# SwiGLU: two plain blocks' weights asked for before the first product's blocks, and the second product's weights asked for nine pieces ahead

## The chip, the cores and the metric

The kernel runs on one core of a Trainium2 chip, in one launch. The metric is the device time of that core in microseconds. Before the change three runs took 1242.67, 1244.71 and 1245.03 us, median 1244.71 us. A further execution was profiled: it took 1243.57 us, and its records span 1241.0 us; every row below is from that one.

## The reference

The model is a trunk of two layers on 512 positions of 1024 features in float32: a recurrent mixer (RG-LRU) with a SwiGLU, then a dilated windowed attention with a second SwiGLU. The change touches the two SwiGLUs alone, each of which computes, with a hidden width of 2816:

```python
def swiglu(h, w_in, w_out):
    g, u = jnp.split(h @ w_in, 2, axis=-1)
    return (jax.nn.silu(g) * u) @ w_out

h = h + swiglu(rms_norm(h, a_ffn_norm[i]), a_ffn_w_in[i], a_ffn_w_out[i])
```

## The kernel before

**Engines.** TensorE (PE) multiplies. Each float32 product is done as three matmuls of 128x512 (L163, L164, L165) on operands that were split into a high and a low part: a weight piece lands in a raw tile wr, ScalarE (ACT) casts the high part into wh (L117), and VectorE (DVE) subtracts to get the low part wl (L124). SyncE (SP) issues nearly all loads and GpSimd (POOL) the adding loads; both, like ACT and DVE, work through their instructions in the written order.

**The stream of pieces.** All weights are one list of pieces, numbered through the whole program. `ws.get(i)` hands out the split parts of piece i; before that, `prefetch(i)` asks for the loads of all pieces up to i + `al`, and splits all up to i + `asp`. There are two raw tiles wr and three pairs wh, wl; so the load of a piece waits until the piece two loads before it has been split, and its split waits until PE has finished with the piece three before it. `load_to(i)` asks for loads up to piece number i of the whole program and does nothing when they have been asked for.

**One SwiGLU** (`swiglu`, called for both layers, f1 and f2). Of the hidden blocks, two (four pieces: two gates, two ups) go the plain way; I call these plain pieces p0 to p3 in their order. The other 20 go through a scheme of seven products in five rounds, q0 to q4, whose raw weights lie in tiles GA, GB, S1, S3 and UB that `fetch` loads (two loads of 512 KB each; S1 and S3 get a second pair, added by POOL, L638). The text ORDERS says in which order the products (GA.B11 and so on), the blocks of the second product ("O", weights f_out) and the split of the round before's results ("L", `parts_of`) stand. In q1 to q3 it is S1, GA, GB, L, S2, O, O, S3, O, S4, O, UB. I call the four second-product pieces of a round O1 to O4. A product takes two pieces of the list (they have no load of their own, since they are split from GA and the like), an O one. `land` (L718) moves a round's results with 16 small DMAs after UB.

**At the start** of a SwiGLU, p0 and p1 were already asked for by the stage before. The normalization needs the sum of squares ssum (L288), which PE adds up (L296) after p0; DVE makes a reciprocal root and diagonals dgh and dgl from it (L298 to L308); PE spreads them over the partitions (L314, L315) after p1; ACT copies the result, rb (L316), and then p2, p3 and GA follow on PE. The block of code around L776 to L788 writes the order of SP, ACT, DVE, POOL and PE by hand, except that splits have a higher priority and may be placed earlier. The tiles of `fetch` lie where the stage before had its own, so the first fetch waits for the end of that stage's work (ssum).

## Time and profile before

| | PE | DVE | ACT | POOL |
|---|---|---|---|---|
| busy, us | 1167.8 | 852.6 | 624.4 | 189.3 |
| share of the span (1241.0 us; this execution's time 1243.57 us) | 94% | 69% | 50% | 15% |

The two SwiGLUs lie at about 151 to 510 us and 862 to 1241 us of the span. The page gives, for each engine, its busy time, and for each pair of instruction and cause how long the engine sat idle until that cause came. A time is worth something only where PE, the busiest engine, waits; so the idle time of PE and its clock are what to look at. Matmuls overlap: one of 128x512 is listed with 0.39 us but the next starts some 0.23 us later.

### The profile page before, as it was taken

What the parts mean: (1) busy time and instruction counts of PE and PEld (TensorE: products, weight loads), DVE (VectorE), ACT (ScalarE), POOL (GpSimd) and SP (SyncE); (2) the same over time, 40 slices, a digit from 0 to 9 for tenths busy, and PEclk for the clock granted to TensorE, in tenths of its full rate; (3) what the DMA queues carried; (4) which work ended last, traced back from release to release, by engine and by line L of the source; (5) the groups of instructions that cost most, each with busy time, mean ns of one, the idle gap of its engine ahead of it and who ended that gap; (6) DMA issues with size and microseconds to landing.
All of it is one profiled execution on the core that took longest, in us unless ns stands there. A gap on an engine that the chain in (4) does not pass through costs nothing.

```text
span 1241.0 us, 15125 instructions
## 1 busy us (share of the span) xinstructions
PE 1167.8 (94%) x5403; PEld 960.5 (77%) x5403; DVE 852.6 (69%) x1525; ACT 624.4 (50%) x901; POOL 189.3 (15%) x221
## 2 busy tenths in 40 slices
PE   9999929999999999999999999999299999999998
PEld 6788827878787788888888888898278787878887
DVE  8987527886757587787564676756378667675864
ACT  6796315553524353575555677645255535352522
POOL 4210010110101000010411343340101101010000
PEclk9999979999999999999999999999699999999999
DMA  7643190884655632432978567434808756465324
GB/s 242 133 119 106 64 288 1 218 237 123 192 147 175 164 103 63 124 112 89 226 178 177 128 142 165 98 72 106 252 20 226 195 153 186 132 181 146 106 70 130
DMA packets 92234, 179.61 MB, mean 145 GB/s; under 512 B 8704, under 2 KB 27008, under 8 KB 92160
## 3 DMA queue, kind: packets, MB, share of 16 engines
q1 hardware_dynamic: 72144, 130.23, 31.8%
q0 software_dynamic: 18864, 47.19, 21.6%
q10 hardware_dynamic: 1152, 1.23, 0.3%
q8 instruction: 43, 0.70, 0.2%
q14 instruction: 31, 0.25, 0.1%
HBM read 164.99 MB, written 2.10 MB: 135 GB/s over the span
## 4 chain that ended last, share of the span: by engine, by line
PE 78%; DVE 8%; DMA 7%; ACT 4%; issue 2%; SPq 1%; POOL 0%; ACTq 0%; DVEq 0%
PE ps L164 21%; PE ps L165 21%; PE ps L163 20%; PE ps L1031 5%; PE ps L1032 5%; PE ps L1033 5%; DMA wr<-in_f_out 3%; DMA wr<-in_f_in 2%; DVE wl L653 1%; DMA GB<-in_f_in 1%; ACT wh L117 1%; ACT wh L652 1%; PE ps L1110 1%; PE ps L1197 1%; DVE xc L449 1%
## 5 line engine op out<-in xcount | busy, mean ns | idle before, releaser
L117 ACT CAST wh<-wr 128x1024 fp32r<-128x1024 f32 (+2 forms) x136 | 131.7, 969 | 191.7 <-PE ps L164 83.4
L124 DVE TENSOR_TENSOR wl<-wr,wh 128x1024 fp32r<-128x1024 f32 (+2 forms) x93 | 100.5, 1084 | 80.4 <-ACT wh L117 80.0
L163 PE MATMUL ps<-gh,wh 128*128 128x512 f32 x288 | 117.3, 407 | 14.5 <-ACT wh L117 14.5
L164 PE MATMUL ps<-wl,xh 128*128 128x512 f32 x320 | 125.0, 391 | 1.9 <-DVE wl L653 1.9
L163 PE MATMUL ps<-wh,xh 128*128 128x512 f32 x320 | 124.7, 390 | 0.0
L165 PE MATMUL ps<-wh,xl 128*128 128x512 f32 x320 | 124.6, 390 | 0.0
L164 PE MATMUL ps<-gl,wh 128*128 128x512 f32 x288 | 118.1, 410 | 0.8 <-issue 0.5
L165 PE MATMUL ps<-gh,wl 128*128 128x512 f32 x288 | 118.0, 410 | 0.1
L638 POOL DMA_DIRECT2D S<-in_f_in x40 | 48.4, 1270 | 420.1 <-DMA S<-in_f_in 140.2
L163 PE MATMUL ps<-xh,wh 128*128 128x512 f32 x256 | 102.3, 401 | 0.8 <-ACT xh L274 0.8
L164 PE MATMUL ps<-xl,wh 128*128 128x512 f32 x256 | 101.2, 395 | 0.1
L652 ACT CAST wh<-S 128x1024 fp32r<-128x1024 f32 x60 | 63.0, 1050 | 75.6 <-PE ps L164 30.3
L165 PE MATMUL ps<-xh,wl 128*128 128x512 f32 x256 | 100.9, 394 | 0.0
L653 DVE TENSOR_TENSOR wl<-S,wh 128x1024 fp32r<-128x1024 f32 x60 | 73.1, 1222 | 32.7 <-ACT wh L652 32.7
L165 PE MATMUL ps<-wh,T 128*128 128x512 f32 x240 | 93.5, 390 | 0.0
L164 PE MATMUL ps<-wl,T 128*128 128x512 f32 x240 | 93.5, 390 | 0.0
L163 PE MATMUL ps<-wh,T 128*128 128x512 f32 x240 | 93.5, 390 | 0.0
L1031 PE MATMUL ps<-wh,xh 128*128 128x512 f32 x224 | 91.5, 408 | 0.0
L1033 PE MATMUL ps<-wh,xl 128*128 128x512 f32 x224 | 87.7, 392 | 0.0
L1032 PE MATMUL ps<-wl,xh 128*128 128x512 f32 x224 | 87.4, 390 | 0.0
L769 DVE TENSOR_TENSOR h<-h,ps 128x512 f32<-128x512 f32 x64 | 43.5, 686 | 60.8 <-PE ps L165 60.8
L163 PEld LDWEIGHTS ps<-gh,wh 128*128 128x128 f32 x288 | 56.2, 195 | 29.6 <-ACT wh L117 17.1
(284 smaller groups left out, 2684.9 us busy)
## 6 DMA issues: line engine op xcount, KB each, us to landing
S<-in_f_in SPq DMA_DIRECT2D x40, 512.0 KB, 4.6
S<-in_f_in POOLq DMA_DIRECT2D x40, 512.0 KB, 7.5
wr<-in_f_out SPq DMA_DIRECT2D x36, 512.0 KB, 5.7
wr<-in_w_q SPq DMA_DIRECT2D x28, 512.0 KB, 6.8
wl<-in_w_q POOLq DMA_DIRECT2D x28, 512.0 KB, 7.5
GA<-in_f_in SPq DMA_DIRECT2D x20, 512.0 KB, 4.5
GB<-in_f_in SPq DMA_DIRECT2D x20, 512.0 KB, 4.6
UB<-in_f_in SPq DMA_DIRECT2D x20, 512.0 KB, 5.9
```

The source lines that it names most:

```text
L117: nc.scalar.copy(hi[:, c], r[:, c])
L124: a = eng.tensor_tensor(lo[:, c], r[:, c], hi[:, c].bitcast(F32), ALU.subtract)
L163: PE.matmul(ps, wh, xh, start=first, stop=False, skip_group_check=on)
L164: PE.matmul(ps, wh, xl, start=False, stop=False, skip_group_check=on)
L165: PE.matmul(ps, wl, xh, start=False, stop=last, skip_group_check=on)
L638: nc.gpsimd.dma_start(c, p.part(1, q, n == "S1", i), accum_op=ALU.add)
L652: S.copy(hi, r)
L653: V.tensor_tensor(lo, r, hi.bitcast(F32), ALU.subtract)
L769: V.tensor_tensor(by_time(x), by_time(x), in_turn(ps), ALU.subtract)
L1031: PE.matmul(ps[t], xh[k][:, r], wh[:, c], start=k == 0, stop=False)
L1032: PE.matmul(ps[t], xh[k][:, r], wl[:, c], start=False, stop=False)
L1033: PE.matmul(ps[t], xl[k][:, r], wh[:, c], start=False, stop=k == 7)
```

## The change

`load_to` gets the numbers of p2 and p3, where it had 2 and 3, numbers of the whole list that had long been loaded. So p2 is asked for ahead of GA, and p3 between GA and GB. Loads are asked for nine pieces ahead, and four again from the first product of the last round on.

```diff
         def swiglu(fp, p, after, meanwhile=iter(())):
-            ws.asp, ws.al = 2, 4
+            ws.asp, ws.al = 2, 9
...
             with tc.manual_schedule(engines={E.PE, E.DVE, E.Activation, E.SP, E.Pool}):
-                ws.load_to(2)
+                ws.load_to(p.steps[2][3])
                 fetch(0, "GA")
-                ws.load_to(3)
+                ws.load_to(p.steps[3][3])
                 for n in ("GB", "S1", "S3", "UB"):
                     fetch(0, n)
                 for s, (kind, *what) in enumerate(p.steps):
+                    if kind == "product" and what[0] == len(ORDERS) - 1:
+                        ws.al = 4
                     {"plain": plain_block, "product": product, "out": out_block, "parts": parts_of}[kind](*what)
```

First place: SP at the start of f1. wr_1291 and wr_1328 are p0 and p1, the next two loads from f_in into wr are p2 and p3; S_ is S1, then S3. Before:

```order
L100 DMA wr_1291<-in_f_in 128x1024
L100 DMA wr_1328<-in_f_in 128x1024
L636 DMA GA<-in_f_in 128x2x512 x2
L636 DMA GB<-in_f_in 128x2x512 x2
L636 DMA S_1387<-in_f_in 128x2x512 x2
L636 DMA S_1392<-in_f_in 128x2x512 x2
L636 DMA UB<-in_f_in 128x2x512 x2
L100 DMA wr_1401<-in_f_in 128x1024
L100 DMA wr_1403<-in_f_in 128x1024
L93 DMA wr_1600<-in_f_out 128x4x256
```

And of the changed kernel, at the same place of SP:

```order
L100 DMA wr_1291<-in_f_in 128x1024
L100 DMA wr_1328<-in_f_in 128x1024
L100 DMA wr_1381<-in_f_in 128x1024
L636 DMA GA<-in_f_in 128x2x512 x2
L100 DMA wr_1386<-in_f_in 128x1024
L636 DMA GB<-in_f_in 128x2x512 x2
L636 DMA S_1391<-in_f_in 128x2x512 x2
L636 DMA S_1396<-in_f_in 128x2x512 x2
L636 DMA UB<-in_f_in 128x2x512 x2
L93 DMA wr_1405<-in_f_out 128x4x256
```

p2 and p3 have moved from behind the ten loads of fetch to places before GA and behind it; round q0's first second-product piece follows directly. SP has the same difference at the start of f2.

Second place: DVE at the end of the stage ahead of f1. h_71 is the last of the eight tiles of the residual stream. Before:

```order
L533 TENSOR_TENSOR h_71<-h_71,ps 128x512
L275 SCALAR_TENSOR_TENSOR xl<-h_71,par,xh 128x512
L288 TENSOR_TENSOR ssum<-ssum,sq 128x512
L124 TENSOR_TENSOR wl_1410<-wr_1401,wh_1409 128x1024
L595 TENSOR_TENSOR wt<-h_64 128x256
```

And changed:

```order
L533 TENSOR_TENSOR h_71<-h_71,ps 128x512
L124 TENSOR_TENSOR wl_1412<-wr_1381,wh_1411 128x1024
L275 SCALAR_TENSOR_TENSOR xl<-h_71,par,xh 128x512
L288 TENSOR_TENSOR ssum<-ssum,sq 128x512
L595 TENSOR_TENSOR wt<-h_64 128x256
```

The split of p2 has moved ahead of the last low part xl and the last addition to ssum; on ACT its cast has moved ahead of the last xh in the same way. The rest of DVE, ACT, POOL and PE stands in the same order in both kernels.

Third place: SP from the end of round q0 through q1 of f1. The gl rows are `land`, GA and the rest the fetches for q2, the wr rows O1 to O4 of q1. Before:

```order
L718 DMA gl<-wt 32x4x128 x12
L636 DMA GA<-in_f_in 128x2x512 x2
L636 DMA S_2066<-in_f_in 128x2x512 x2
L93 DMA wr_2088<-in_f_out 128x2x512
L93 DMA wr_2106<-in_f_out 128x2x512
L93 DMA wr_2180<-in_f_out 128x2x512
L636 DMA S_2220<-in_f_in 128x2x512 x2
L93 DMA wr_2272<-in_f_out 128x2x512
L636 DMA GB<-in_f_in 128x2x512 x2
```

And changed:

```order
L93 DMA wr_1949<-in_f_out 128x2x512
L718 DMA gl<-wt 32x4x128 x12
L93 DMA wr_1991<-in_f_out 128x2x512
L636 DMA GA<-in_f_in 128x2x512 x2
L93 DMA wr_2065<-in_f_out 128x2x512
L636 DMA S_2072<-in_f_in 128x2x512 x2
L93 DMA wr_2144<-in_f_out 128x2x512
L636 DMA S_2222<-in_f_in 128x2x512 x2
L636 DMA GB<-in_f_in 128x2x512 x2
```

O1 has moved ahead of `land`, O2 ahead of GA, O3 ahead of the fetch of S1, O4 ahead of that of S3. With two raw tiles, O3 now stands in SP's queue until O1 has been split, and the fetch of S1 stands behind it. The same holds for q2 and q3, and in f2.

## The prediction

> **What bounds the kernel now.** I read the page first, then the waits of PE, the chain of waits, and PE, DVE, ACT and SP in order of time around PE's gaps. From the page, and from the waits of PE (what waited for what: us in total, times, the longest):

> ```profile
> PE 1167.8 (94%) x5403; PEld 960.5 (77%) x5403; DVE 852.6 (69%) x1525; ACT 624.4 (50%) x901; POOL 189.3 (15%) x221
> PEclk9999979999999999999999999999699999999999
> ...
> PE ps L314 <- DVE dgh L307: 43.8, 2, 21.9
> PE ps L163 <- ACT wh L117: 14.5, 6, 2.8
> PE ps L164 <- DVE wl L653: 1.9, 2, 0.9
> ```

> PE is the bound, so only its idle time and its slow clock can be won. Two waits of 21.9 us, one at the start of each SwiGLU, and six of 2.4 us on a cast make 58 us. The clock row dips in the two slices with the long ones. The chain of waits (start, us, what) shows where a long one comes from:

> ```profile
> 161.64 13.83 DMA wr<-in_f_in
> 175.83 1.05 ACT wh L117
> 176.90 1.23 DVE wl L124
> 178.13 1.34 DVE wt L595 x4
> ...
> 185.14 0.77 PE ps L314
> 186.37 0.58 ACT rb L316
> ...
> 204.02 1.15 DVE wl L653
> ...
> 894.97 0.77 PE ps L314
> 896.20 0.58 ACT rb L316
> ```

> L314 needs the diagonals from DVE, and DVE stands at wl of p2, whose load was issued at 161.64 behind ten loads and landed at 175.5. The diagonals need nothing of p2; from the end of wl (178.1) DVE takes 7 us to the last of them, at 185.1. f2 repeats these rows 709.8 us later.

> PE in order of time (start, us; in brackets the idle time and its end) at two of the short waits, O1 of q1 in f1 and of q3 in f2, the first and the last of the six:

> ```profile
> 270.51 0.39 PE L165 MATMUL ps<-wh,T 128*128 128x512 f32 x1
> 273.67 0.49 PE L163 MATMUL ps<-gh,wh 128*128 128x512 f32 x1 [2.77 <-ACT wh L117]
> 274.33 0.76 PE L164 MATMUL ps<-gl,wh 128*128 128x512 f32 x1 [0.17 <-issue]
> 277.91 0.39 PE L163 MATMUL ps<-gh,wh 128*128 128x512 f32 x1
> ...
> 1114.11 0.80 PE L163 MATMUL ps<-gh,wh 128*128 128x512 f32 x1 [2.75 <-ACT wh L117]
> 1117.77 0.39 PE L165 MATMUL ps<-gh,wl 128*128 128x512 f32 x1
> ```

> A wait costs more than its idle time. The nine matmuls from 273.67 to 277.91 took 4.24 us where nine usually take 9 x 0.23 = 2.05: a stretch at half clock that costs 2.2 us. The last wait's eight matmuls took 3.66 in place of 1.82, 1.8 more. The six come to 12.7 us of this; in what follows one such stretch is 2.1 us.

> **The change part by part: the start.** SP and DVE around the stage's end (first SP, then DVE):

> ```profile
> 131.83 5.76 SPq L100 DMA_DIRECT2D wr<-in_f_in  x2
> 154.35 0.90 SPq L636 DMA_DIRECT2D GA<-in_f_in  x2
> ...
> 141.45 1.23 DVE L124 TENSOR_TENSOR wl<-wr,wh 128x1024 fp32r<-128x1024 f32 x1 [0.21 <-ACT wh L117]
> 151.43 0.69 DVE L533 TENSOR_TENSOR h<-h,ps 128x512 f32<-128x512 f32 x1 [2.05 <-PE ps L165]
> 153.58 0.69 DVE L288 TENSOR_TENSOR ssum<-ssum,sq 128x512 f32<-128x512 f32 x1
> ```

> p2's load follows p0's and p1's on SP and waits for p0's raw tile, free when p0 is split (141.45 + 1.23 = 142.7). No other load runs then; it lands near 148. Its cast needs the wh that PE leaves at about 151.4, so it runs at 151.4 to 152.4, ahead of the last xh, and its wl ahead of the last xl and ssum: the split that cost DVE a 22.6 us wait now costs 0.7 us at ssum (near 155.0, was 154.3). That delay is hidden, since PE multiplies p0 up to 156.7 and only then reads ssum. From 155.0 DVE needs the same 7 us to the last diagonal: 162.0. PE ends p1 at 185.14 - 21.92 = 163.2, so L314 no longer waits, with 1 us to spare; f2 repeats the rows, and its working leaves less to spare, but some.

> With PE never idle, L314 also runs at full clock: from its start to rb 0.66 us (one matmul's 0.23, the other's listed 0.39, a handover) in place of 1.23. So rb comes 21.9 + 0.6 = 22.5 us earlier.

> What is late next: from rb on, ACT and DVE make T2, T3, the split of GA and of GB, and PE already waits for their last step now:

> ```profile
> 203.80 0.48 PE L163 MATMUL ps<-wh,xh 128*128 128x512 f32 x1
> 205.22 0.50 PE L164 MATMUL ps<-wl,xh 128*128 128x512 f32 x1 [0.94 <-DVE wl L653]
> ```

> That chain (186.37 to 205.17, 18.8 us, its order unchanged) ends 22.5 us earlier, and PE goes on then. PE itself reaches this point still earlier, because p2 loses its nine half-clock matmuls (1.85 us); so its idle time there grows from 1.2 to 1.2 + 1.85 - 0.6 = 2.5 us. The growth is already in the 22.5, but the six rows above had a slow stretch after 2.2 us or more, and these two rows none after 1.2. I charge 2.1 us for a new slow stretch. Start: 2 x (22.5 - 2.1) = **40.8 us**.

> Can other loads come too late? p3 now is third in the queue behind GA. Loads by issue time (KB, us to landing), GA and behind it GB, whose first load was third, then the page's second-product pieces and the added loads:

> ```profile
> GA<-in_f_in SPq DMA_DIRECT2D x2, 512.0 KB, 4.2
> GB<-in_f_in SPq DMA_DIRECT2D x2, 512.0 KB, 6.7
> ...
> wr<-in_f_out SPq DMA_DIRECT2D x36, 512.0 KB, 5.7
> S<-in_f_in POOLq DMA_DIRECT2D x40, 512.0 KB, 7.5
> ```

> GB was issued at 155.3; p3 with ssum's 0.7 us lands near 162.5 and is cast before rb at 163.9. GA, GB, S1, S3 and UB lie at most one 512 KB load and 0.7 us later than before; round q0's first O is the tail of the queue in p3's old place (landed by about 178) and is wanted at 205.5 - 22.5 = 183. I cost these at nothing; without this cover p3's delay would go one to one into rb.

> **The second product.** O1 of q1 to q3 was issued behind the fetches of GA and S1 and landed some 5.7 us after; now it is issued ahead of `land`, O2 directly behind. All six waits on DMA end. The idle time is 14.5 us by the list, plus 0.16 each since the listed 0.39 of the last matmul is longer than its 0.23: 15.5; with the slow stretches 28.2 us. What stands next is ACT's and DVE's order: gh and gl (L724, L725) before O1's split. In q4 the weights were there in time already (ACT, DVE, PE):

> ```profile
> 464.35 1.04 ACT L117 CAST wh<-wr 128x1024 fp32r<-128x1024 f32 x1
> 465.43 1.23 DVE L124 TENSOR_TENSOR wl<-wr,wh 128x1024 fp32r<-128x1024 f32 x1
> 466.71 0.50 PE L165 MATMUL ps<-gh,wl 128*128 128x512 f32 x1
> ```

> There PE loses 0.2 us at L165 (466.28 to 466.71 in place of 0.23). I give that to q3 of f1 and q1 to q3 of f2: 0.8. In f1 the rotary tables stand on DVE between gl and O1's wl, in q1 and q2:

> ```profile
> 270.33 0.35 DVE L868 TENSOR_SCALAR grow<-grow 128x384 f32<-128x384 f32 x1
> 272.13 0.29 DVE L879 SCALAR_TENSOR_TENSOR rtmp<-rtmp 128x128 f32<-128x128 f32 x1
> ...
> 335.87 0.22 DVE L922 TENSOR_SCALAR cc<-rtmp 128x128 f32<-128x128 f32 x1
> 336.09 0.39 PE L165 MATMUL ps<-wh,T 128*128 128x512 f32 x1
> ```

> In q1 DVE is free at 272.4 and wl ends at 273.6; PE, done with S2 at 270.74, wants it with its third matmul at 271.2. So 2.4 us of this wait stay, as a wait on DVE, with its slow stretch: 4.5. In q2 wl ends near 337.25, wanted at 336.32 + 0.46: 0.5. Left in all 5.8. Second product: 28.2 - 5.8 = **22.4 us**.

> New waits on SP: O3 blocks S1's fetch until O1 is split.

> ```profile
> 395.56 0.88 SPq L636 DMA_DIRECT2D S<-in_f_in  x2
> 438.84 1.05 ACT L652 CAST wh<-S 128x1024 fp32r<-128x1024 f32 x1 [2.90 <-issue]
> ```

> In q3 that fetch moves from 395.6 to some 401.7, 6 us; with a landing of 5.7 and POOL's added loads of 7.5 (rows above) it is complete before 420, and ACT reads it at 438.8. Hidden by some 20 us.

> **Sum.** 40.8 + 22.4 = 63.2 us off the profiled execution's 1243.57 (2.6 us around its span of 1241.0): 1180.4. The median of the three runs is 1.1 us above that execution; I take **1181**.

> [...] The rows show half clock after idle times of 2.2 to 2.9 us. [...]

> **Rivals.**
> - *No new slow stretch.* If the 2.5 us at GB's split, or the 2.4 in q1, leaves the clock alone, as the 1.2 us did: up to 3 x 2.1 less, 1175. For it: the rows end at 1.2 and begin at 2.2. Against it: six of six above that were slow. 0.22.
> - *p3 late.* ACT holds rb behind p3's cast. If p3 shares the engines with the eight loads behind it instead of keeping its place, it may land 3 us after rb's time: 2 x 3, 1187. Against it: GA's pair landed in 4.2 us (row above) with the same loads behind it. 0.14.
> - *O1's wait changes its name everywhere.* If DVE's wl is as late in all six as in q1, 4.5 stay in each: 27 in place of 5.8, 1202. Against it: q4's rows. 0.06.
> - *The start doesn't move.* The two raw tiles keep p2's load from going ahead, or its early place in ACT and DVE stalls the stage before: 40.8 lost, 1222. Against it: p0's tile is free at 142.7. 0.04.
> - *Slower.* SP in order: S1 behind O3 must come later than 438.8 by more than the gain. It would need the 20 us of cover gone and another 11 us of PE idle in each of six rounds (63.2/6), to reach 1245 and above. It decides only if O1's split came 30 us later. 0.02.

> The forecast has 0.52. 1172 to 1191 takes in the forecast, the first two rivals and some us of unlisted small waits either way. A measurement of this kernel tells some 0.2% (2.5 us) from no change; all but the last rival are far beyond: faster 0.97, same 0.01, slower 0.02.

> **What would show it.** L314's wait gone from PE's waits, and L163 on ACT wh L117 nearly so; L164 on DVE wl L653 with two waits near 2.3 us by the list; a new L165 on DVE wl L124 of about 2 us in q1 of f1; p2's cast at about 151.4; slow stretches left at three places. Wrong if PE waits for S or GA casts, or if rb stands well behind L315.

## The result and the profile after

The changed kernel takes 1176.78 us (median of four runs, 1175.40 to 1178.36) beside 1244.85 us before: a ratio of 0.9457, 95% interval 0.9441 to 0.9474, some 68 us less. It is inside the range and 4 us below the forecast of 1181. The profiled execution took 1176.97 us, with a span of 1175.0 us.

From the page of the changed kernel, busy time and the granted clock in 40 slices, and from its waits of PE (what waited for what: us, times, the longest):

```profile
PE 1155.8 (98%) x5403; PEld 952.7 (81%) x5403; DVE 850.7 (72%) x1525; ACT 623.3 (53%) x901; POOL 189.6 (16%) x221
PEclk9999999999999999999999999999999999999999
...
PE ps L164 <- DVE wl L653: 2.4, 3, 1.0
PE ps L163 <- ACT wh L652: 2.2, 2, 1.1
PE ps L165 <- DVE wl L124: 1.9, 2, 1.6
```

PE's share rises from 94% to 98%, and the two slices with a low clock are gone. Neither L314 nor the cast at L117 is in the list; what stands there is the chain of ACT and DVE ahead of GB at the start (the first two rows, but for one wait of 0.55 us on L653 in q1 of f1) and O1's split in q1 and q2 of f1 (the third).

The start of f1 in the changed kernel, SP, ACT and DVE in order of time:

```profile
131.59 11.21 SPq L100 DMA_DIRECT2D wr<-in_f_in  x3
154.68 0.90 SPq L636 DMA_DIRECT2D GA<-in_f_in  x2
155.62 0.46 SPq L100 DMA_DIRECT2D wr<-in_f_in  x1
...
151.01 1.05 ACT L117 CAST wh<-wr 128x1024 fp32r<-128x1024 f32 x1 [3.24 <-issue]
161.18 1.06 ACT L117 CAST wh<-wr 128x1024 fp32r<-128x1024 f32 x1 [4.31 <-DMA wr<-in_f_in]
163.48 0.59 ACT L316 COPY rb<-ps 128x512 f32<-128x512 f32 x1 [1.24 <-PE ps L315]
...
152.10 1.23 DVE L124 TENSOR_TENSOR wl<-wr,wh 128x1024 fp32r<-128x1024 f32 x1 [0.22 <-ACT wh L117]
153.90 0.69 DVE L288 TENSOR_TENSOR ssum<-ssum,sq 128x512 f32<-128x512 f32 x1
161.40 0.35 DVE L308 SCALAR_TENSOR_TENSOR dgl<-ident,nry,dgh 128x128 fp32r<-128x128 f32 x1
```

p2 is cast at 151.0 without a wait for its load; the diagonals are done at 161.8, and PE's p1 ends at 162.8. p3's load, issued at 155.6, lands at 161.2, and ACT is done with its cast 1.2 us before rb can be copied. rb comes at 163.5, was 186.4.

PE at the place that is late next, GB's first piece, and at O1 of q1 (the bracket is the idle time and its end):

```profile
179.38 0.39 PE L165 MATMUL ps<-wh,xl 128*128 128x512 f32 x1
180.88 0.50 PE L163 MATMUL ps<-wh,xh 128*128 128x512 f32 x1 [1.12 <-ACT wh L652]
182.33 0.50 PE L164 MATMUL ps<-wl,xh 128*128 128x512 f32 x1 [0.95 <-DVE wl L653]
...
248.83 0.49 PE L163 MATMUL ps<-gh,wh 128*128 128x512 f32 x1
249.47 0.47 PE L164 MATMUL ps<-gl,wh 128*128 128x512 f32 x1
251.51 0.51 PE L165 MATMUL ps<-gh,wl 128*128 128x512 f32 x1 [1.58 <-DVE wl L124]
253.29 0.63 PE L165 MATMUL ps<-gh,wl 128*128 128x512 f32 x1
```

From 179.38 to 182.33 there are two starts, 2.95 us where 0.46 is usual: 2.5 us lost, in two pieces. At O1 the third matmul waits; behind it a stretch of matmuls of 0.63 us stands for half clock: the granted clock was 0.50 from 252.67 to 256.08. This is the only one left in this execution but for the last 0.75 us of the span, where PE is idle.

### The profile page after: what moved, and what is told of

It reads as the page before. It is cut to its first block, busy times and chain, and to the rows that moved or that the text cites. A ratio compares the mean times of both kernels' runs of the same rounds, so it can differ in the third digit from the quotient of the medians.

```text
span 1175.0 us, 15128 instructions
## 1 busy us (share of the span) xinstructions
PE 1155.8 (98%) x5403; PEld 952.7 (81%) x5403; DVE 850.7 (72%) x1525; ACT 623.3 (53%) x901; POOL 189.6 (16%) x221
## 3 DMA queue, kind: packets, MB, share of 16 engines
q10 hardware_dynamic: 1152, 1.23, 0.4%
## 4 chain that ended last, share of the span: by engine, by line
PE 83%; DVE 6%; DMA 5%; ACT 3%; issue 2%; SPq 1%; POOL 0%; ACTq 0%; DVEq 0%
PE ps L165 22%; PE ps L164 22%; PE ps L163 22%; PE ps L1033 5%; PE ps L1034 5%; PE ps L1035 5%; DMA wr<-in_f_out 2%; DMA S<-in_f_in 1%; PE ps L1112 1%; PE ps L1199 1%; ACT wh L117 1%; DMA UB<-in_f_in 1%; DVE wl L653 1%; DMA GB<-in_f_in 1%; DVE xc L449 1%
## 5 line engine op out<-in xcount | busy, mean ns | idle before, releaser
L117 ACT CAST wh<-wr 128x1024 fp32r<-128x1024 f32 (+2 forms) x136 | 131.2, 969 | 138.5 <-PE ps L164 82.8
L164 PE MATMUL ps<-wl,xh 128*128 128x512 f32 x320 | 124.9, 390 | 2.4 <-DVE wl L653 2.4
L163 PE MATMUL ps<-wh,xh 128*128 128x512 f32 x320 | 124.8, 390 | 2.2 <-ACT wh L652 2.2
L165 PE MATMUL ps<-wh,xl 128*128 128x512 f32 x320 | 124.6, 389 | 0.0
L165 PE MATMUL ps<-gh,wl 128*128 128x512 f32 x288 | 115.2, 400 | 2.1 <-DVE wl L124 1.9
L163 PE MATMUL ps<-gh,wh 128*128 128x512 f32 x288 | 114.4, 397 | 0.4 <-DVE e L695 0.4
L124 DVE TENSOR_TENSOR wl<-wr,wh 128x1024 fp32r<-128x1024 f32 (+2 forms) x93 | 99.9, 1083 | 20.6 <-ACT wh L117 20.2
L164 PE MATMUL ps<-gl,wh 128*128 128x512 f32 x288 | 114.4, 397 | 0.1
L652 ACT CAST wh<-S 128x1024 fp32r<-128x1024 f32 x60 | 63.0, 1050 | 73.7 <-PE ps L165 28.9
L163 PE MATMUL ps<-xh,wh 128*128 128x512 f32 x256 | 101.4, 398 | 0.5 <-ACT xh L274 0.5
L164 PE MATMUL ps<-xl,wh 128*128 128x512 f32 x256 | 99.9, 390 | 0.1
L165 PE MATMUL ps<-xh,wl 128*128 128x512 f32 x256 | 99.9, 390 | 0.0
L653 DVE TENSOR_TENSOR wl<-S,wh 128x1024 fp32r<-128x1024 f32 x60 | 73.1, 1222 | 30.6 <-ACT wh L652 30.6
L163 PE MATMUL ps<-wh,T 128*128 128x512 f32 x240 | 93.5, 389 | 0.0
L165 PE MATMUL ps<-wh,T 128*128 128x512 f32 x240 | 93.5, 389 | 0.0
L164 PE MATMUL ps<-wl,T 128*128 128x512 f32 x240 | 93.5, 389 | 0.0
L164 PEld LDWEIGHTS ps<-wl,xh 128*128 128x128 f32 x320 | 60.1, 188 | 16.0 <-DVE wl L653 3.5
## 6 DMA issues: line engine op xcount, KB each, us to landing
S<-in_f_in SPq DMA_DIRECT2D x40, 512.0 KB, 6.6
S<-in_f_in POOLq DMA_DIRECT2D x40, 512.0 KB, 8.9
wr<-in_f_out SPq DMA_DIRECT2D x36, 512.0 KB, 5.3
wr<-in_w_q SPq DMA_DIRECT2D x28, 512.0 KB, 6.7
wl<-in_w_q POOLq DMA_DIRECT2D x28, 512.0 KB, 7.5
GA<-in_f_in SPq DMA_DIRECT2D x20, 512.0 KB, 4.9
GB<-in_f_in SPq DMA_DIRECT2D x20, 512.0 KB, 6.3
UB<-in_f_in SPq DMA_DIRECT2D x20, 512.0 KB, 5.3
```

The source lines that it names most:

```text
L117: nc.scalar.copy(hi[:, c], r[:, c])
L124: a = eng.tensor_tensor(lo[:, c], r[:, c], hi[:, c].bitcast(F32), ALU.subtract)
L163: PE.matmul(ps, wh, xh, start=first, stop=False, skip_group_check=on)
L164: PE.matmul(ps, wh, xl, start=False, stop=False, skip_group_check=on)
L165: PE.matmul(ps, wl, xh, start=False, stop=last, skip_group_check=on)
L652: S.copy(hi, r)
```

## The experiments

Each kernel is the changed one with the edit shown. The first four ran on one chip, beside 1246.34 us for the kernel before (median of seven runs); the other four on another, beside 1246.55 (nine runs).

**The start alone.** Loads four ahead, as before the change.

```diff
-            ws.asp, ws.al = 2, 9
+            ws.asp, ws.al = 2, 4
```

> The start alone (loads four ahead, as before). My theory: the two parts add, and each of the two long waits gives 22.5 us without a new slow stretch: 1243.6 - 45 = 1198.6 us; L163 on ACT wh L117 stays near 14.5 us in six waits, each with its stretch at half clock of about 2.1 us. Rival, the parts overlap (a start that is earlier also lets the second product's loads come in time): near 1177 us and no waits on L117. Rival, the second product's part carried most of it: above 1215 us.

Measured: 1201.56 us (1197.13 to 1204.11), ratio 0.9631, interval 0.9602 to 0.9660: 46.0 us less by the ratio (42.4 to 49.6), 44.8 by the medians. Its waits of PE:

```profile
PE ps L163 <- ACT wh L117: 15.8, 6, 3.3
PE ps L163 <- ACT wh L652: 2.2, 2, 1.1
PE ps L164 <- DVE wl L653: 1.9, 2, 1.0
```

All six waits at O1 stay, and both at the start are gone. It is 3 us above what I expected, and the profiled execution has a slow stretch at GB of f1 (granted clock 0.50 from 184.19 on) that the expectation left out. The parts don't overlap; the start carries two thirds.

**Nine pieces ahead alone.** p2 and p3 asked for behind the fetches.

```diff
-                ws.load_to(p.steps[2][3])
+                ws.load_to(2)
                 fetch(0, "GA")
-                ws.load_to(p.steps[3][3])
+                ws.load_to(3)
```

> Loads nine ahead alone, p2 and p3 behind the fetches as before. My theory: the second product's 22.4 us, so 1221 us; the two waits of 21.9 us on DVE dgh L307 stay whole; one wait of about 2 us on DVE wl L124 (q1 of f1) with one slow stretch in place of six. Rival, overlap: more than 1235 us or less than 1210 us.

Measured: 1220.49 us (1219.07 to 1221.21), ratio 0.9794, interval 0.9775 to 0.9812: 25.7 us less (23.4 to 28.0). Its waits of PE:

```profile
PE ps L314 <- DVE dgh L307: 43.1, 2, 21.7
PE ps L165 <- DVE wl L124: 1.9, 2, 1.6
```

The long waits stay whole, the six short ones are gone but for the one on DVE. The slow stretch that I expected there wasn't in this execution (its mean granted clock was 0.982, in the three others 0.980), which is 2 us of the 3 that it is better than said. The two parts alone add to 71.7 us, together they measured 67.6 (65.5 to 69.6): they add, within the intervals, though an overlap of a few us isn't excluded.

**p3 behind the fetches.** Is it only p2 that matters, as the long wait's name says?

```diff
-                ws.load_to(p.steps[3][3])
                 for n in ("GB", "S1", "S3", "UB"):
                     fetch(0, n)
+                ws.load_to(p.steps[3][3])
```

> As changed, but p3 is asked for behind all the fetches again; p2 stays early. My theory: ACT holds rb behind p3's cast; p3 lands near 177 us, so rb moves from 163.5 to about 178, 14.5 us later in each SwiGLU, and PE idles some 9 us ahead of p3 and more at GA and GB, with slow stretches: 1177 + 29 + 2 to 8, about 1208 to 1214 us. L314's wait stays gone. Rival (only p2 matters, since the diagonals need only DVE): 1177 us, no new wait.

A single run: 1207.75 us. ACT, then PE, at the start of f1:

```profile
177.75 1.04 ACT L117 CAST wh<-wr 128x1024 fp32r<-128x1024 f32 x1 [20.31 <-DMA wr<-in_f_in]
178.71 0.58 ACT L316 COPY rb<-ps 128x512 f32<-128x512 f32 x1
...
178.85 0.79 PE L163 MATMUL ps<-xh,wh 128*128 128x512 f32 x1 [9.39 <-ACT wh L117]
```

rb stands behind p3's cast in ACT's order, 15 us later, though PE had spread the diagonals long before; PE idles 9.4 us ahead of p3. So with p2 early and p3 not, 31 us of the start's 46 are given back (32 beside the next run, on the same chip). The rival falls.

**Both ahead of GA.** Was there still something to win from p3?

```diff
-                fetch(0, "GA")
                 ws.load_to(p.steps[3][3])
+                fetch(0, "GA")
```

> As changed, but p3 is asked for ahead of GA too. My theory: p3 was in time already, so nothing moves: 1175 to 1179 us, rb within 0.2 us of 163.5. Rival (p3 still holds rb up by a little in the changed kernel): 1 to 3 us faster, rb earlier.

A single run: 1175.78 us. rb comes 8.81 us after the issue of GA (155.18 to 163.99), in the changed kernel 8.80 (154.68 to 163.48). Nothing moved: p3's place behind GA costs nothing.

**The rotary tables later.** They no longer take a step right behind L, so O1's split follows gl on DVE.

```diff
-                    if s > 12:
+                    if s > 12 and kind != "parts":
                         next(meanwhile, None)
```

> As changed, but the rotary tables' steps aren't taken right behind L, so O1's wl in q1 of f1 stands directly behind gl on DVE. My theory (what is left there is DVE's order): the wait on DVE wl L124 falls from 1.9 to about 0.2 us, in q2 too, and the slow stretch at this place is gone: 2 us idle and up to 1.7 of slow clock, so 1173 to 1175 us beside 1176.8 of the changed kernel. Rival (O1's load, or gh on ACT, is late as well): the wait takes another name and the time stays within 1 us.

Measured: 1175.28 us (five runs, 1174.02 to 1176.74), ratio 0.9427, interval 0.9410 to 0.9445. DVE in q1 of f1:

```profile
247.52 2.50 DVE L725 TENSOR_TENSOR gl<-gl,gh 128x512 fp32r<-128x512 f32 x4 [1.31 <-ACT gh L724]
250.04 2.36 DVE L124 TENSOR_TENSOR wl<-wr,wh 128x1024 fp32r<-128x1024 f32 x2
```

The wait on wl L124 falls to 0.16 us, in q1 and in q2, and there is no slow stretch at that place; so the wait was DVE's order and nothing behind it. In time it is 1.3 us by the medians, and the intervals of this run and of the changed kernel beside it overlap; that execution had a slow stretch at GB of f1 instead (granted clock 0.50 from 184.30 on).

**GA's split earlier, too.** The run before, with T2 and T3 made one step later and their low parts between two steps of the plain pair.

```diff
-            def plain_pair(j):
+            def plain_pair(j, between=lambda: None):
...
                 V.scalar_tensor_tensor(w, plain[HB + j], -1.0, rows[0], ALU.mult, ALU.mult)
+                between()
...
-            early = {1: make_t23, 2: lambda: (low_t23(), plain_pair(0)), 3: lambda: plain_pair(1),
+            early = {2: lambda: (make_t23(), plain_pair(0, low_t23)), 3: lambda: plain_pair(1),
```

> As the run before, and GA's first split ahead of T2 and T3 on ACT and DVE, with T2's and T3's low parts between two steps of the plain pair where DVE waits for ACT. My theory (at GB PE waits for a chain of ACT and DVE from rb on, 18.8 us long, in which DVE idles 5 us): the chain shortens by about 2 us, GB's wait in each SwiGLU falls from 2.5 to below 1 us and never slows the clock: 4 us less plus 0 to 4 for slow stretches, about 1169 us. Rival (GB's weights or ps late from elsewhere): no change.

Measured: 1170.99 us (1168.54 to 1173.13), ratio 0.9397, interval 0.9376 to 0.9417. Its waits of PE at GB and O1:

```profile
PE ps L164 <- DVE wl L653: 0.4, 2, 0.2
PE ps L165 <- DVE wl L124: 0.2, 1, 0.2
```

GB's waits fall from 2.1 to 0.2 us by the list in each SwiGLU. The interval ends below that of the changed kernel on the same chip (0.9422), so this one is faster than the changed kernel, by 5.6 us by the medians; I expected 1169. Beside the run before it is 4.3 us by the medians, with intervals that overlap.

**The changed kernel again.**

> The changed kernel again, for the runs beside it on the same chip and for another phase of the clock: about 1177 us. The waits are the same as in the first profile to 0.1 us. If the clock falls after any window of 3.41 us of a free-running grid in which PE idles more than half, the slow stretches at GB of f1 and f2 and at O1 of q1 come and go from one execution to the next, 0 to 3 of them. If the length of a wait decides, they are the same as in the first profile: one, at O1 of q1.

Measured: 1176.57 us (1174.22 to 1178.49), ratio 0.9441, interval 0.9422 to 0.9461. PE at GB of f1:

```profile
182.29 0.50 PE L163 MATMUL ps<-wh,xh 128*128 128x512 f32 x1 [1.11 <-ACT wh L652]
183.74 0.50 PE L164 MATMUL ps<-wl,xh 128*128 128x512 f32 x1 [0.95 <-DVE wl L653]
184.89 0.63 PE L165 MATMUL ps<-wh,xl 128*128 128x512 f32 x1
```

These waits and the one at O1 of q1 are those of the first profile to 0.02 us (one at GB of f2 is 0.13 longer), yet here GB's of f1 are followed by half clock (0.50 from 184.63 on), and O1 of q1, with the same wait of 1.6 us, is not. So in these two executions the length of the wait doesn't settle it.

**A longer wait.** gl of the plain pair computed twice.

```diff
                     halve(plain["w"], *(x[:, 2:4] for x in chunks[0]))
+                    V.tensor_tensor(chunks[0][1][:, 2:4], plain["w"], chunks[0][0][:, 2:4].bitcast(F32), ALU.subtract)
```

> As changed, with the plain pair's low part gl computed twice on DVE, so GB's split comes 1.15 us later and PE idles 3.6 us there, in two pieces of about 1.3 and 2.3 us. Grid theory: whatever the phase, one of the windows holds some 1.8 us or more, so both GB waits now are followed by a slow stretch: 1177 + 2.3 + 2 to 4 us, near 1182. Length theory (2.2 us in one piece): the same here, so this run counts only against a theory by which such waits don't slow the clock at all: 1179 us.

A single run: 1181.69 us. Both waits at GB are followed by half clock: in f1 one stretch of 3.4 us (granted clock 0.50 from 184.19 on), in f2 one of 6.8 (from 863.45 on). That speaks against the theory that such waits leave the clock alone.

## Why the prediction was right

**The long waits at the start: right, cause and size.** p2's load behind ten others, held in DVE's order, was the cause: asked for earlier, the wait is gone whole (43.8 us to none), and with the nine-ahead part alone it stays whole. The forecast had 45.0 us for both before any new slow stretch; the start alone gave 46.0 (42.4 to 49.6). rb was forecast at 163.9 and came at 163.5.

**p3's cover: right.** It was forecast to land near 162.5 and be cast before rb; it landed at 161.2. That this step isn't free when p3 is late was argued from ACT's order and is shown by the run that put it behind: 31 us. One cover was thinner than forecast: q0's first O, the tail of the queue, was to land by about 178 and be wanted at 183; it was issued at 163.06 and landed 19.3 us later, at 182.4, and ACT took it up at 182.64. Nothing was lost, but it was close.

**What is late next: right in place and size.** 2.5 us at GB, forecast 2.5 and measured 2.5 in f1; that it is the chain from rb is shown by the kernel that shortens it, where it goes. The name was forecast less well: not one wait of 2.3 us on DVE wl L653 but two, 1.1 on ACT wh L652 and 0.95 on L653.

**The slow stretch at GB: mis-sized.** I charged 2.1 us in each SwiGLU, since all six waits of 2.2 us and more had been followed by one. In the profiled execution there was none, in the second profile one, in the three others with the same waits one each, in f1 or in f2 (from 184.19, 184.30 and 860.29 on). The 4.2 us of this term are more than the 3.4 us between the sum, 1180.4, and the 1176.97 that the execution took; without them the sum is 1176.2. It was the rival named "no new slow stretch", with 0.22, that came nearest for this execution; over several it is in part the one, in part the other. The 2.1 us are a little much, too: the stretch of 3.41 us at half clock at O1 of q1 would cost half of it, 1.7 us, by estimate, and 1.6 were measured. The rest was the slow first matmul behind a wait (273.67 to 274.33, 0.4 us more than usual), which the changed kernel has at O1 as well (248.83 to 249.47).

**The second product: right.** 22.4 us were forecast, with 4.5 left at q1 of f1, 0.5 at q2, 0.2 elsewhere; alone it gave 25.7. Left in the profiled execution are 2.0 - 0.2 = 1.8 us at the third matmul and 0.5 us at the two before, with a slow stretch of 1.6 us (13 starts from 251.85 to 256.19): 3.9; at q2 0.5. The cause given for q1, the rotary steps ahead of wl on DVE, is shown by the run that moves them. Two small waits weren't listed ahead: 0.4 us on DVE e L695 within O1 of q0 in f2, and 0.55 on DVE wl L653 in q1 of f1, which the second profile doesn't have.

**SP's new order: hidden, with less cover than said.** SP and ACT of the changed kernel in q3 of f1:

```profile
374.90 0.37 SPq L93 DMA_DIRECT2D wr<-in_f_out  x1
375.37 2.50 SPq L636 DMA_DIRECT2D S<-in_f_in  x2
...
407.84 1.05 ACT L652 CAST wh<-S 128x1024 fp32r<-128x1024 f32 x1 [2.90 <-issue]
```

O3 and the fetch of S1 behind it go out at 375, directly after O1's split. Before, S1 went 43.3 us ahead of ACT's reading it (395.56 to 438.84), now 32.5; ACT waits for it no more than before (2.90 us of issue in both). POOL's two added loads go out from 381.70 on, and the later one lands at 394.0, 13.8 us ahead of the reading, where some 20 were forecast. The forecast brought the fetch 6 us nearer to its reading, and it came 10.8 nearer: O1's wait and its slow stretch lay between O1's split and the reading, and they are gone as well.

## What to carry to other kernels

A wait is named after the instruction that came last, not after what held that one: here the matmul waited for diagonals, which waited in DVE's order behind a split that needed an unrelated load. So follow a wait back through the in-order engine to the first thing that waited for data, and look at what is queued on the other engine too: p3's load is in no wait of the kernel before, and would have taken back nearly half the gain. When a stall goes, work out when the next chain ends from the same start, and count a slow stretch behind a wait as a chance, not a price: behind the same two waits at GB, some 2.1 us together, one came at four places of ten in five executions here.

## What the runs showed of the hardware

The same two waits at GB of f2, in the changed kernel and in the one with both pieces ahead of GA, each over two steps of its own grid (length, PE busy and count, then the weight load, DVE, ACT and POOL, the granted clock, and the share of the DMAs and their GB/s). The changed kernel, whose low stretch ends at 256.08, 176 steps of 3.4133 us ahead of the first row:

```profile
856.83:860.24 3.41, 2.31 (x11) 1.58 (x9) 2.19 (x3) 2.65 (x4) 0.00 (x0) 1.00 1.11 231
860.24:863.65 3.41, 2.44 (x10) 1.80 (x10) 2.54 (x3) 1.88 (x3) 0.00 (x0) 1.00 1.12 230
```

And the one with both ahead of GA:

```profile
856.88:860.29 3.41, 1.35 (x6) 0.67 (x5) 2.98 (x3) 3.41 (x6) 0.00 (x0) 1.00 1.11 232
860.29:863.70 3.41, 3.41 (x10) 2.67 (x9) 1.74 (x2) 0.82 (x1) 0.00 (x0) 0.50 0.47 110
```

Both lose some 2.07 us of PE's busy time. Split over two steps, 1.10 and 0.97, it left the clock at 1.00; within one step, 2.06, it was followed by a step at 0.50. In the executions before and after, counted in the same way, eleven steps at full clock were followed by half clock: one with 1.72 us of idle PE (changed kernel, from 249.25), the others with 2.0 to 3.41. One with 1.83 us (before, from 161.64) was not, nor was any other, with 1.36 us at most. So these two executions give no single idle time that divides them.

A step at half clock was followed by full clock, in the same two executions, where PE idled 0.15 us or less in it (nine steps), and by another at half clock where PE idled 2.88 us or more (eleven). Between the two lies the stretch at GB of f2 in the kernel with the longer wait, which lasted two steps: the second of its two waits ran on into the low step (3.41 - 2.43 = 0.98 us idle there).

```profile
860.03:863.45 3.42, 1.07 (x4) 0.34 (x2) 2.66 (x3) 3.42 (x5) 0.00 (x0) 1.00 1.11 232
863.45:866.86 3.41, 2.43 (x6) 1.95 (x7) 2.06 (x2) 0.34 (x2) 0.00 (x0) 0.50 0.96 207
866.86:870.27 3.41, 3.41 (x10) 2.64 (x9) 1.23 (x1) 1.58 (x2) 0.00 (x0) 0.50 0.03 10
```

Open is what else spreads the runs of one kernel by 2 to 7 us: the kernel with no more than 0.2 us of wait at GB and O1 still spans 1168.5 to 1173.1, with no slow stretch in the one execution of it that was profiled.
